# Weights split later and attention steps at new positions, and wide matmuls ahead of narrow ones

## The chip, the cores and the metric

One NeuronCore of a Trainium2 chip runs the whole program in one launch. The metric is the device time of one execution in microseconds; the median of three runs is given, and one execution was profiled.

## The reference

An encoder trunk of two layers on 256 tokens of 1024 channels, in float32. Each layer has a half-step SwiGLU FFN, a token-mixing sub-layer and a second FFN, each between two RMSNorms.

```python
for l in range(DEPTH):                                    # DEPTH = 2
    x = x + 0.5 * rmsnorm(swiglu(rmsnorm(x, g), w_gate, w_up, w_down), g2)   # D_FF = 2816
    x = x + rmsnorm(token_mixing(rmsnorm(x, g), w_in, ..., w_out), g2)
    x = x + 0.5 * rmsnorm(swiglu(rmsnorm(x, g), w_gate, w_up, w_down), g2)

def token_mixing(h, ...):                                 # heads of 64 channels
    qa, ka, va, qb, kb, vb, qc, kc, vc = split(h @ w_in)
    o_a = softmax over a band of chunks + a learned bias  # group A, 6 heads
    o_b = softmax1 - lam * softmax2, then rmsnorm         # group B, 4 heads, lam from 4 small vectors
    o_c = stick-breaking weights                          # group C, 6 heads
    return concat(o_a, o_b, o_c) @ w_out

# stick-breaking: z = q k^T / 8, strictly causal
a = exp(log_sigmoid(z) + reversed_cumsum(log_sigmoid(-z)) - log_sigmoid(-z))
```

## The kernel before

**Precision.** A float32 product is made of three products of float32r halves: every weight chunk is split into `whi` (a cast, on ScalarE, line 139) and `wlo` (raw minus `whi`, on VectorE, line 140), and activations are held as two such halves in `xT`. `mm3` issues high x high, high x low and low x high. In `cols_pair` the two high products are one matmul of 512 columns (`xT` holds both halves side by side, line 405), and the low one is a matmul of 256 columns into the second half of the same PSUM bank (line 407); ScalarE and VectorE then add the halves of the bank.

**The weights' stream.** `Stream` takes the chunks (512 KB as a rule) in the order in which they are used. Four raw buffers are filled by DMAs on SyncE's queue, nine pairs of split buffers hold halves. `stream.ahead(n)` cuts up to `n` half chunks (a cast and a subtraction each), as far as a split buffer is free; when a chunk is cut, its raw buffer is free and the load of the chunk four later is issued. `stream.done()` frees a split pair.

**An FFN.** Two column pairs are done with the tokens on the rows (`gate`, `up`), the nine others with `cols_pair`: gate and up, each with two banks of 8 wide and 8 narrow matmuls. `down` then accumulates 22 chunks into four banks tagged `acc`, three matmuls of 512 columns per product.

**Token mixing.** First the values of the three groups (`values`), then 16 column tiles `pp_0` to `pp_15` of queries and keys (groups B, C, A in turn), each 8 x 3 matmuls of 256 columns, lines 373 to 375. A tile has four quarters of 6 matmuls; quarter q of tile f ends slot 4f + q. After each slot the program issues the steps of the heads that have a position in that slot, and then goes on with the tile. `PLAN` holds these positions, so the order on every engine is written out by this table. The down projection continues the slots from 64 on. The engines run their own instructions strictly in this order and wait for each other by semaphores.

- `qk`: the copy of tile f out of PSUM by ScalarE into `qkT` (`evacuate`, lines 841 and 843).
- `b`: steps of a head of group B: scores `s_b` and softmax for two maps (line 720 on VectorE, 722 on ScalarE), the combination (line 765), transposes `pT_b` on TensorE, their copy `wT_b`, the output `o_b`, its scaling.
- `c`: steps of a pair of heads of group C: scores `s_c` and masked adds (lines 668 and 670) twice, three activations (672 to 674), the combination with the maximum (676) on VectorE, two casts (682, 683) and two differences (684, 685), prefix sums `u_c` on TensorE, two subtractions (697, 698), an exponential (700), the outputs `o_c`, their split `yC`.
- `a`: steps of a pair of heads of group A: scores `s_a`, softmax, scaling, transposes `pT_a`, copies, outputs `o_a`, split.
- `sub`, `turn`, `bias`, `lambda`, `gain`, `table`: the norm of group B's outputs, its transposes, the bias of group A (line 637), lambda (lines 592 to 597), a load and a table of ScalarE.
- `pieces`: entry n is the argument of `stream.ahead` at n + 0.9.
- `acc`: between which positions a PSUM tile of a kind is taken from the `acc` banks (four) and not from the four tagged `rot`, which the column tiles use too.

Of the kernel before, what the change touches and what calls it, by code (L numbers as in the profile page):

```python
# [19 lines left out]
KT = D // P  # L20
# [17 lines left out]

PLAN = {
    "qk": [  # L40
        7.05, 7.1, 14.05, 16.05, 19.05, 23.05, 27.05, 33.05, 35.05, 39.05, 43.05, 47.05, 53.05, 55.05,
        59.05, 63.05
    ],
# [5 lines left out]
    ],  # L49
# [4 lines left out]
    ],  # L54
    "a": [
        [49.1, 49.25, 51.05, 55.05, 57.05, 60.05, 62.05],
        [57.15, 58.35, 59.1, 64.1, 65.05, 68.05, 69.25],
        [65.1, 66.05, 67.05, 72.05, 72.1, 77.05, 78.05],
    ],
    "sub": [  # L60
        55.1, 64.05
    ],
    "turn": [
        [66.15, 66.2],
        [69.2, 69.3],
    ],
    "pieces": [
        1, 0, 0, 1, 2, 0, 3, 0, 0, 2, 1, 0, 2, 0, 0, 4, 0, 0, 0, 4, 0, 0, 2, 2, 2, 1, 0, 2, 4, 3, 1, 1, 1,
        3, 0, 4, 0, 3, 1, 1, 0, 3, 2, 1, 1, 1, 2, 3, 1, 3, 3, 3, 1, 0, 0, 0, 3, 1, 1, 1, 1, 4, 2, 0
    ],  # L70
    "bias": 41.05,
    "lambda": 11.05,
    "gain": 81.1,
    "table": 82.05,
    "tail": 5,
    "acc": {"pT": [14, 26], "oB": [-10, 40], "oC": [-36, -14], "sA": [-140, 58]},
}
NSPLIT = 9

# [82 lines left out]
def trunk_kernel(  # L162
# [55 lines left out]
    stream = Stream(nc, raw_pool, split_pool)  # L218
# [177 lines left out]
    def cols_pair(out, c, nm, between=lambda: None):  # L396

        for j in range(2):  # L400
            cs = slice(j * P, j * P + P)
            ps = psum.tile([P, 2, SEQ], F32, tag="rot", name=f"{nm}_{j}")
            for k in range(KT):
                wh, wl = stream.get(c + k // 4)
                nc.tensor.matmul(ps.rearrange("p a t -> p (a t)"), lhsT=wh[:, k % 4, cs],  # L405
                                 rhs=xT[:, k].rearrange("p a t c -> p (a t c)"), start=k == 0, stop=False)
                nc.tensor.matmul(ps[:, 1, :], lhsT=wl[:, k % 4, cs], rhs=xT[:, k, 0].rearrange("p t c -> p (t c)"),  # L407
                                 start=False, stop=k == KT - 1)
            if j == 0:
                between()  # L410
            side = work.tile([P, 512], F32, tag="tc", bufs=3, name=f"side_{nm}_{j}")[:, :SEQ]
            nc.scalar.copy(side, ps[:, 1, :])  # L412
            nc.vector.tensor_add(out[:, j, :], ps[:, 0, :], side)  # L413
# [54 lines left out]
    def ffn(i, turn1):  # L468
# [74 lines left out]
        for f in range(4, KF, 2):  # L543
            cc = stream.used

            def close():
                while closing:
                    token_close(*closing.pop())

            sg = work.tile([P, 512], F32, tag="ta", bufs=TA, name=f"sg{i}_{f}")  # L550
            cols_pair(sg.rearrange("p (a b) -> p a b", a=2), cc, f"pg{i}_{f}", close)
            nc.scalar.activation(sg, sg, AF.Silu)
            stream.done(2)
            stream.ahead(6)
            h = work.tile([P, 512], F32, tag="tb", bufs=3, name=f"h{i}_{f}")
            hv = h.rearrange("p (a b) -> p a b", a=2)
            cols_pair(hv, cc + 2, f"pu{i}_{f}")
            nc.vector.tensor_mul(h, sg, h)
            split_copy(hT_hi(f, 2), hT_lo(f, 2), hv)
            stream.done(2)  # L560
            stream.ahead(6)
# [13 lines left out]
    def mix(i, l, turn1):  # L575
# [27 lines left out]
        c = stream.used  # L603
# [20 lines left out]
        values(2, 0)  # L624
        values(2, 1)
        stream.done(2)
        stream.ahead(6)
        qkT = act.tile([P, 16, SEQ], F32, tag="bigh1", name=f"qkT{l}")
        yb = act.tile([P, 2816], F32, tag="bigl1", name=f"yb{l}")
        yB = yb[:, :512].rearrange("p (t d) -> p t d", t=2)  # L630
# [298 lines left out]
    for i in range(3 * DEPTH):  # L929
        turn1 = mix(i, i // 3, turn1) if i % 3 == 1 else ffn(i, turn1)  # L930
# [36 lines left out]
```

## Time and profile before

| | |
|---|---|
| median of 3 runs | 1020.4 us (1018.77 to 1021.05) |
| the profiled execution | 1022.65 us |
| its span, first to last instruction | 1020.7 us |
| mean granted clock of TensorE | 0.991 |
| busy: TensorE, VectorE, ScalarE | 996.7, 672.3, 586.4 us |
| loaded | 181.08 MB, 178 GB/s over the span |

Times in rows are microseconds from the span's start. A row of the timeline has start, length, engine, line, operation, tiles, shapes and count, and in brackets how long the engine had been idle and which instruction ended that. "PE" is TensorE's matmuls, "DVE" VectorE, "ACT" ScalarE. A matmul's length includes its drain, so the rows of TensorE overlap, and two starts tell more than one length. The engines' lengths overlap a little, too.

### The profile page before, as it was taken

The numbers are of one execution on the slowest core, as the hardware profiler recorded it, in microseconds if no ns is written. First come the engines' busy times: TensorE is split into PE (matmuls) and PEld (weight loads), VectorE is DVE, ScalarE is ACT, GpSimd is POOL, SyncE is SP. The second block draws the span as 40 slices with busy tenths as digits, with TensorE's granted clock in tenths as the row PEclk, the third lists the DMA queues.
The fourth block names the chain that finished last, engine by engine and source line by source line (L and its number), as shares of the span: only waits on it lengthen the run. The fifth ranks groups of instructions, "written<-read, shape, count | busy, mean of one in ns | idle before, by whom it ended". The sixth has DMA issues, their size and how long they took to land.

```text
span 1020.7 us, 16031 instructions
## 1 busy us (share of the span) xinstructions
PE 996.7 (98%) x5940; PEld 874.6 (86%) x5940; DVE 672.3 (66%) x1345; ACT 586.4 (57%) x1265; POOL 43.2 (4%) x73
## 2 busy tenths in 40 slices
PE   8899999999999999999999999999989999999997
PEld 7788888899887988888899888888978789888886
DVE  4576675577686577765557767646678756866642
ACT  5465564466766566555446756545577655765531
POOL 3100000010000100000020000001000010000000
PEclk8999999999999999999999999999999999999999
DMA  8866656748344477656726865663853525765631
GB/s 265 234 201 181 196 171 228 199 131 235 101 145 124 145 219 217 185 201 210 223 69 206 249 197 173 227 192 118 253 150 105 158 90 175 240 202 189 215 114 41
DMA packets 151005, 183.16 MB, mean 179 GB/s; under 512 B 5744, under 2 KB 134896, under 8 KB 150928
## 3 DMA queue, kind: packets, MB, share of 16 engines
q1 hardware_dynamic: 148448, 174.08, 55.7%
q0 software_dynamic: 2192, 7.54, 2.5%
q8 instruction: 46, 0.75, 0.3%
q10 hardware_dynamic: 288, 0.52, 0.1%
q14 instruction: 31, 0.25, 0.1%
HBM read 181.08 MB, written 1.05 MB: 178 GB/s over the span
## 4 chain that ended last, share of the span: by engine, by line
PE 83%; DVE 5%; DMA 5%; ACT 4%; issue 1%; POOL 0%; SPq 0%; DVEq 0%; POOLq 0%; ACTq 0%
PE pg L405 13%; PE pu L405 13%; PE acc L373 9%; PE acc L375 9%; PE acc L374 9%; PE pg L407 7%; PE pu L407 7%; DVE wlo L140 3%; DMA raw<-in_w_in_dram 2%; PE pp L373 2%; DMA raw<-in_ffn_w_up_dram 2%; PE pp L375 2%; PE pp L374 1%; ACT p_b L722 1%; PE pu L374 1%
## 5 line engine op out<-in xcount | busy, mean ns | idle before, releaser
L140 DVE TENSOR_TENSOR wlo<-raw,whi 128x512 fp32r<-128x512 f32 (+1 forms) x625 | 395.6, 688 | 157.1 <-ACT whi L139 156.8
L139 ACT CAST whi<-raw 128x512 fp32r<-128x512 f32 x630 | 349.8, 617 | 122.0 <-PE acc L375 71.3
L405 PE MATMUL pg<-xT,whi 128*128 128x512 f32 x576 | 207.1, 401 | 0.0
L405 PE MATMUL pu<-xT,whi 128*128 128x512 f32 x576 | 205.2, 399 | 0.0
L407 PE MATMUL pg<-xT,wlo 128*128 128x256 f32 x576 | 162.3, 282 | 0.0
L407 PE MATMUL pu<-xT,wlo 128*128 128x256 f32 x576 | 161.8, 281 | 0.0
L373 PE MATMUL acc<-whi,hh 128*128 128x512 f32 x352 | 137.2, 390 | 0.0
L374 PE MATMUL acc<-wlo,hh 128*128 128x512 f32 x352 | 137.0, 389 | 0.0
L375 PE MATMUL acc<-whi,hl 128*128 128x512 f32 x352 | 137.0, 389 | 0.0
L405 PEld LDWEIGHTS pg<-xT,whi 128*128 128x128 f32 x576 | 108.9, 189 | 26.7
L405 PEld LDWEIGHTS pu<-xT,whi 128*128 128x128 f32 x576 | 108.2, 188 | 27.0
L407 PEld LDWEIGHTS pg<-xT,wlo 128*128 128x128 f32 x576 | 109.5, 190 | 0.0
L407 PEld LDWEIGHTS pu<-xT,wlo 128*128 128x128 f32 x576 | 108.8, 189 | 0.0
L375 PEld LDWEIGHTS acc<-whi,hl 128*128 128x128 f32 x352 | 66.1, 188 | 13.9
L373 PEld LDWEIGHTS acc<-whi,hh 128*128 128x128 f32 x352 | 66.1, 188 | 13.6
L374 PEld LDWEIGHTS acc<-wlo,hh 128*128 128x128 f32 x352 | 66.1, 188 | 13.4
L373 PE MATMUL pp<-xT,whi 128*128 128x256 f32 x256 | 76.4, 298 | 0.0
L374 PE MATMUL pp<-xT,whi 128*128 128x256 f32 x256 | 73.0, 285 | 0.0
L375 PE MATMUL pp<-xT,wlo 128*128 128x256 f32 x256 | 73.0, 285 | 0.0
L412 ACT COPY side_pu<-pu 128x256 f32<-128x256 f32 x72 | 26.1, 368 | 50.3 <-PE pu L407 50.3
L373 PEld LDWEIGHTS pp<-xT,whi 128*128 128x128 f32 x256 | 49.4, 193 | 4.9 <-issue 4.2
L413 DVE TENSOR_TENSOR h<-pu,side_pu 128x256 f32<-128x256 f32 x72 | 29.8, 422 | 30.4 <-ACT side_pu L412 30.2
(247 smaller groups left out, 1455.1 us busy)
## 6 DMA issues: line engine op xcount, KB each, us to landing
raw<-in_ffn_w_gate_dram SPq DMA_DIRECT2D x88, 512.0 KB, 4.8
raw<-in_ffn_w_up_dram SPq DMA_DIRECT2D x88, 512.0 KB, 4.6
raw<-in_ffn_w_down_dram SPq DMA_DIRECT2D x88, 512.0 KB, 4.4
raw<-in_w_in_dram SPq DMA_DIRECT2D x36, 512.0 KB, 5.3
raw<-in_w_out_dram SPq DMA_DIRECT2D x16, 512.0 KB, 3.5
raw<-in_w_in_dram SPq DMA_DIRECT2D x8, 576.0 KB, 4.3
gpost<-in_ffn_post_g_dram POOLq DMA_DIRECT2D x4, 512.0 KB, 4.3
raw<-in_w_in_dram SPq DMA_DIRECT2D x4, 384.0 KB, 3.4
```

Of the source, the lines that this page charges most:

```text
L139: self.nc.scalar.copy(self.hi[:, a:b], raw[:, a:b])
L140: (lo or self.nc.vector).tensor_sub(self.lo[:, a:b], raw[:, a:b], self.hi.bitcast(F32)[:, a:b])
L373: nc.tensor.matmul(ps, lhsT=ah, rhs=bh, start=first, stop=False)
L374: nc.tensor.matmul(ps, lhsT=ah, rhs=bl, start=False, stop=False)
L375: nc.tensor.matmul(ps, lhsT=al, rhs=bh, start=False, stop=last)
L405: nc.tensor.matmul(ps.rearrange("p a t -> p (a t)"), lhsT=wh[:, k % 4, cs], rhs=xT[:, k].rearrange("p a t c -> p (a t c)"), start=k == 0, ...
L407: nc.tensor.matmul(ps[:, 1, :], lhsT=wl[:, k % 4, cs], rhs=xT[:, k, 0].rearrange("p t c -> p (t c)"), start=False, stop=k == KT - 1)
L412: nc.scalar.copy(side, ps[:, 1, :])
L413: nc.vector.tensor_add(out[:, j, :], ps[:, 0, :], side)
L722: nc.scalar.activation(p[:, a:b], p[:, a:b], AF.Exp, bias=st[:, t : t + 1], scale=-1.0, accum_out=st[:, 2 + t : 3 + t])
```

## The change

Three things are changed. In `cols_pair` the 8 wide matmuls of a bank come first and the 8 narrow ones after them. Ahead of the column tiles of token mixing, `stream.ahead(2)` stands for `stream.ahead(6)`. In `PLAN` nearly all positions are new, `pieces` asks for 36 halves where it asked for 88, and the transposes of groups A and B take `rot` banks throughout.

```diff
@@ PLAN
     "qk": [
-        7.05, 7.1, 14.05, 16.05, 19.05, 23.05, 27.05, 33.05, 35.05, 39.05, 43.05, 47.05, 53.05, 55.05,
+        3.05, 7.05, 11.05, 15.05, 19.05, 23.05, 27.05, 31.05, 35.05, 39.05, 43.05, 47.05, 51.05, 55.05,
         59.05, 63.05
     ],
     "b": [
-        [15.02, 15.1, 15.2, 15.3, 15.4, 26.1, 26.25, 30.05, 33.2],
-        [15.05, 15.15, 15.25, 15.35, 15.45, 25.05, 26.05, 33.1, 33.15],
-        [22.05, 22.1, 22.15, 22.2, 22.25, 26.15, 26.2, 30.94, 31.05],
-        [22.07, 22.12, 22.17, 22.22, 22.27, 30.1, 32.05, 44.05, 44.1],
+        [9.1, 9.2, 9.3, 9.4, 9.5, 16.05, 17.05, 20.05, 21.2],
+        [9.12, 9.22, 9.32, 9.42, 9.52, 16.07, 17.07, 20.07, 21.25],
+        [17.1, 17.2, 17.3, 17.4, 17.5, 25.05, 26.05, 29.05, 30.05],
+        [17.12, 17.22, 17.32, 17.42, 17.52, 25.07, 26.07, 29.07, 30.1],
     ],
     "c": [
-        [28.1, 28.15, 28.2, 30.92, 32.1, 39.1, 39.15, 39.2, 42.05, 44.15],
-        [39.25, 39.3, 40.05, 40.1, 44.2, 49.05, 49.15, 49.2, 53.1, 56.05],
-        [43.1, 43.15, 45.05, 45.1, 48.05, 58.05, 58.15, 58.2, 62.15, 62.2],
+        [26.1, 26.15, 26.2, 29.05, 30.15, 34.05, 34.1, 34.15, 38.05, 40.05],
+        [36.1, 36.15, 36.2, 39.15, 40.15, 44.05, 44.1, 44.15, 48.05, 50.05],
+        [45.1, 45.15, 45.2, 48.15, 49.05, 53.05, 53.1, 53.15, 61.05, 62.15],
     ],
     "a": [
-        [49.1, 49.25, 51.05, 55.05, 57.05, 60.05, 62.05],
-        [57.15, 58.35, 59.1, 64.1, 65.05, 68.05, 69.25],
-        [65.1, 66.05, 67.05, 72.05, 72.1, 77.05, 78.05],
+        [50.1, 50.2, 53.2, 56.05, 57.05, 62.05, 63.1],
+        [58.05, 58.2, 60.05, 64.1, 65.05, 68.05, 69.25],
+        [66.05, 66.1, 67.05, 72.05, 72.1, 77.05, 78.05],
     ],
-    "sub": [ 55.1, 64.05 ],
+    "sub": [ 41.1, 46.05 ],
     "pieces": [
...
-    "bias": 41.05,
-    "lambda": 11.05,
+    "bias": 42.05,
+    "lambda": 5.05,
...
-    "acc": {"pT": [14, 26], "oB": [-10, 40], "oC": [-36, -14], "sA": [-140, 58]},
+    "acc": {"pT": [-2, -1], "oB": [-10, 40], "oC": [-36, -14], "sA": [-140, 59]},
@@ cols_pair
             for k in range(KT):
-                wh, wl = stream.get(c + k // 4)
+                wh = stream.get(c + k // 4)[0]
                 nc.tensor.matmul(ps.rearrange("p a t -> p (a t)"), lhsT=wh[:, k % 4, cs],
                                  rhs=xT[:, k].rearrange("p a t c -> p (a t c)"), start=k == 0, stop=False)
+            for k in range(KT):
+                wl = stream.get(c + k // 4)[1]
                 nc.tensor.matmul(ps[:, 1, :], lhsT=wl[:, k % 4, cs], rhs=xT[:, k, 0].rearrange("p t c -> p (t c)"),
                                  start=False, stop=k == KT - 1)
@@ mix
         values(2, 1)
         stream.done(2)
-        stream.ahead(6)
+        stream.ahead(2)
```

The new `pieces` ask for two halves each in the slots 2, 4, 6, 13, 15, 22, 24, 27, 31, 33, 35, 37, 41, 43, 47, 54, 60 and 62, of which the requests of slots 6 and 37 find no free buffer.

On ScalarE, at the start of the column tiles in the first layer, the order before is this (`whi` are casts of weight chunks, `qkT` the copies of column tiles, `lt` the exponential of lambda, `p_b` a softmax of group B):

```order
L139 CAST whi_2361<-raw_2257 128x512 x2
L139 CAST whi_2369<-raw_2291 128x512 x2
L139 CAST whi_2411<-raw_2299 128x512 x2
L841 ACTIVATE qkT_2377<-pp_0_2386 128x256
L843 COPY qkT_2377<-pp_1_2415 128x256
L139 CAST whi_2459<-raw_2307 128x512 x2
L594 ACTIVATE lt_540<-lt_540 128x2
L139 CAST whi_2493<-raw_2367 128x512 x2
L841 ACTIVATE qkT_2377<-pp_2_2446 128x256
L722 ACTIVATE p_b_0_0_2526,st_b_0_0_2527<-p_b_0_0_2526,st_b_0_0_2527 128x128
```

Five chunks and three tiles stood ahead of the first softmax. On the same engine at the same place the order now is this:

```order
L139 CAST whi_2361<-raw_2257 128x512 x2
L139 CAST whi_2397<-raw_2291 128x512 x2
L843 ACTIVATE qkT_2369<-pp_0_2378 128x256
L139 CAST whi_2419<-raw_2299 128x512 x2
L596 ACTIVATE lt_540<-lt_540 128x2
L845 COPY qkT_2369<-pp_1_2412 128x256
L724 ACTIVATE p_b_0_0_2472,st_b_0_0_2473<-p_b_0_0_2472,st_b_0_0_2473 128x128
```

Three chunks, lambda and two tiles stand ahead of it now, and the copy of the second tile stands behind the third chunk and lambda.

On VectorE, from the first to the second pair of group C, the order before is this (`wlo` are low halves of weight chunks, `z_c_0` and `z_c_1` the scores of the first and second pair, `u_c` prefix sums, `s_c` scores in PSUM):

```order
L140 TENSOR_TENSOR wlo_2856<-raw_2611,whi_2855 128x512 x2
L697 TENSOR_TENSOR z_c_0_2756<-z_c_0_2756,u_c_0_2889 128x256
L698 TENSOR_TENSOR z_c_0_2756<-z_c_0_2756,u_c_0_2892 128x512
L668 TENSOR_TENSOR z_c_1_2900<-s_c_1_0_2902,negmask 128x2x128
L670 COPY z_c_1_2900<-s_c_1_0_2902 128x128
L668 TENSOR_TENSOR z_c_1_2900<-s_c_1_1_2907,negmask 128x2x128
L670 COPY z_c_1_2900<-s_c_1_1_2907 128x128
L140 TENSOR_TENSOR wlo_2913<-raw_2695,whi_2912 128x512
L676 SCALAR_TENSOR_TENSOR e_c_1_2901<-z_c_1_2900,e_c_1_2901 128x768
```

The masked adds of the second pair followed the subtractions of the first at once. On the same engine they now stand so:

```order
L140 TENSOR_TENSOR wlo_2820<-raw_2569,whi_2819 128x512 x2
L140 TENSOR_TENSOR wlo_2841<-raw_2696,whi_2840 128x512 x2
L699 TENSOR_TENSOR z_c_0_2744<-z_c_0_2744,u_c_0_2854 128x256
L700 TENSOR_TENSOR z_c_0_2744<-z_c_0_2744,u_c_0_2857 128x512
L140 TENSOR_TENSOR wlo_2873<-raw_2718,whi_2872 128x512 x2
L670 TENSOR_TENSOR z_c_1_2887<-s_c_1_0_2889,negmask 128x2x128
L672 COPY z_c_1_2887<-s_c_1_0_2889 128x128
L670 TENSOR_TENSOR z_c_1_2887<-s_c_1_1_2894,negmask 128x2x128
L672 COPY z_c_1_2887<-s_c_1_1_2894 128x128
L678 SCALAR_TENSOR_TENSOR e_c_1_2888<-z_c_1_2887,e_c_1_2888 128x768
```

Two chunks stand ahead of the subtractions where one stood, and a whole chunk between them and the adds.

More of the change, by code (lines that the diff above doesn't have):

```diff
@@ L44 @@
     "b": [
[4 rows of a table removed]
[4 rows of a table added]
     ],
     "c": [
[3 rows of a table removed]
[3 rows of a table added]
     ],
     "a": [
-        [49.1, 49.25, 51.05, 55.05, 57.05, 60.05, 62.05],
-        [57.15, 58.35, 59.1, 64.1, 65.05, 68.05, 69.25],
-        [65.1, 66.05, 67.05, 72.05, 72.1, 77.05, 78.05],
+        [50.1, 50.2, 53.2, 56.05, 57.05, 62.05, 63.1],
+        [58.05, 58.2, 60.05, 64.1, 65.05, 68.05, 69.25],
+        [66.05, 66.1, 67.05, 72.05, 72.1, 77.05, 78.05],
     ],
     "sub": [
-        55.1, 64.05
+        41.1, 46.05
     ],
@@ L67 @@
     "pieces": [
-        1, 0, 0, 1, 2, 0, 3, 0, 0, 2, 1, 0, 2, 0, 0, 4, 0, 0, 0, 4, 0, 0, 2, 2, 2, 1, 0, 2, 4, 3, 1, 1, 1,
-        3, 0, 4, 0, 3, 1, 1, 0, 3, 2, 1, 1, 1, 2, 3, 1, 3, 3, 3, 1, 0, 0, 0, 3, 1, 1, 1, 1, 4, 2, 0
-    ],
-    "bias": 41.05,
-    "lambda": 11.05,
+        0, 0, 2, 0, 2, 0, 2, 0, 0, 0, 0, 0, 0, 2, 0, 2, 0, 0, 0, 0, 0, 0, 2, 0, 2, 0, 0, 2, 0, 0, 0, 2,
+        0, 2, 0, 2, 0, 2, 0, 0, 0, 2, 0, 2, 0, 0, 0, 2, 0, 0, 0, 0, 0, 0, 2, 0, 0, 0, 0, 0, 2, 0, 2, 0,
+    ],
+    "bias": 42.05,
+    "lambda": 5.05,
     "gain": 81.1,
```

## The prediction

> **What bounds the kernel now.** I read the page's busy times first, then its chain of waits, then the rows of the timeline on the places that the change touches.
>
> ```profile
> PE 996.7 (98%) x5940; PEld 874.6 (86%) x5940; DVE 672.3 (66%) x1345; ACT 586.4 (57%) x1265; POOL 43.2 (4%) x73
> PE 83%; DVE 5%; DMA 5%; ACT 4%; issue 1%; POOL 0%; SPq 0%; DVEq 0%; POOLq 0%; ACTq 0%
> ```
>
> TensorE is the bound (98% busy, 83% of the chain that ended last), so two things count: the spacing of its matmuls, and the places where it waits. Its rows overlap, since each holds its own drain; I therefore read spacing from start to start. These are the first and last rows of a stretch of 12 wide-narrow pairs in the paired columns, of 10 matmuls of 512 columns in the down projection, of 10 of 256 columns in the mixing projection, and the three rows of one prefix sum in which a narrow one, two wide ones and a narrow one follow each other.
>
> ```profile
> 99.73 0.28 PE L407 MATMUL pu<-xT,wlo 128*128 128x256 f32 x1
> 103.97 0.28 PE L407 MATMUL pg<-xT,wlo 128*128 128x256 f32 x1
> ...
> 184.72 0.39 PE L375 MATMUL acc<-whi,hl 128*128 128x512 f32 x1
> 186.98 0.39 PE L373 MATMUL acc<-whi,hh 128*128 128x512 f32 x1
> ...
> 261.76 0.28 PE L374 MATMUL pp<-xT,whi 128*128 128x256 f32 x1
> 262.95 0.28 PE L375 MATMUL pp<-xT,wlo 128*128 128x256 f32 x1
> ...
> 272.07 0.40 PE L691 MATMUL u_c<-h_c,tri 128*128 128x512 f32 x1
> 272.30 0.40 PE L692 MATMUL u_c<-l_c,tri 128*128 128x512 f32 x1
> 272.54 0.39 PE L695 MATMUL u_c<-hl_c,ones_r 128*128 128x256 f32 x2
> ```
>
> A pair in alternation takes (103.97 - 99.73)/12 = 0.353 us. A wide matmul among wide ones takes 2.26/10 = 0.226, a narrow one among narrow ones 1.19/10 = 0.119, together 0.345: alternation costs 0.008 us a pair. At a change of width a wide one takes 0.23 to 0.24, about 0.01 over 0.226.
>
> The other places are the waits of TensorE while the heads run beside the projection, here in the first layer. The first fence has its rows, the second has two windows behind the second wait: stretch, its length, then busy time and instructions of PE, PEld, DVE, ACT and POOL, the granted clock, the DMA share and GB/s.
>
> ```profile
> 249.00 0.28 PE L375 MATMUL pp<-xT,wlo 128*128 128x256 f32 x1
> 250.48 0.53 PE L744 MATMUL s_b<-qkT 32*128 32x128 f32 x8 [1.20 <-ACT qkT L843]
> ...
> 254.78 0.49 PE L729 MATMUL pT_b<-ident,p_b 128*128 128x128 f32 x3
> 257.05 0.74 PE L729 MATMUL pT_b<-ident,p_b 128*128 128x128 f32 x3 [1.78 <-ACT p_b L722]
> ...
> 288.46 0.28 PE L375 MATMUL pp<-xT,wlo 128*128 128x256 f32 x1
> 288.85 0.66 PE L739 MATMUL o_c<-e_c,v 128*64 128x256 f32 x4
> ...
> 291.18 0.49 PE L729 MATMUL pT_a<-ident,p_a 128*128 128x128 f32 x3
> 291.91 0.55 PE L729 MATMUL pT_a<-ident,p_a 128*128 128x128 f32 x3 [0.24 <-ACT qkT L841]
> ```
> ```profile
> 256.00:260.00 4.00, 2.95 (x15) 2.59 (x15) 3.44 (x11) 4.00 (x13) 0.00 (x0) 0.75 0.11 44
> 260.00:264.00 4.00, 4.00 (x30) 3.68 (x30) 2.45 (x6) 1.82 (x4) 0.00 (x0) 0.83 0.62 185
> ```
>
> Start to start less the instruction's own 0.12 (three transposes: 0.33), these waits are 1.36, 1.94, 0.27 and 0.40 us. After the second the clock stood at 0.75 and 0.83 for 4 us each, which is (0.25 + 0.17) x 4 = 1.7 us of work lost. In sum 5.7 us a layer that a better order could give back, and 11.3 over both layers.
>
> **The change part by part.**
>
> *Paired columns.* Per PSUM bank 8 pairs take 8 x 0.353 = 2.83 us. Sorted by width they take 8 x 0.345 = 2.76, and two changes of width add 0.01 each, so 2.78: a gain of 0.046 us. There are 4 FFNs x 9 column pairs x gate and up x 2 = 144 banks: 6.6 us. Its bounds are 0 (if spacing does not depend on the order) and 144 x 0.064 = 9.2 (no price at the changes). I take 6.6, since the prefix sum's rows show that price. The high weight halves are wanted sooner by half a microsecond and the low ones later; no wait stands in any of these rows, and the split runs several chunks ahead, so this costs nothing. If that cover went, the wait would show on the wide matmuls.
>
> In a sentence apart: the Trainium skill, "TensorE: Matmul & The Clock Gate", section "Back-to-back issue gap", gives a gap of N/2.4 + 2.5 ns whatever the neighbour, 216 ns for 512 columns. The trace has 226 and, beside a narrow one, 236 or so, so the rows disagree.
>
> *Splits later.* Counted in the code's tables, 4 halves fewer are cut ahead of the projection, and 36 rather than 88 are asked for during it; the nine buffers grant about as many in both. At the start of a column tile 7 to 9 tiles are still cut ahead, some 20 us of TensorE work (24 matmuls x 0.119 = 2.9 us a tile), so no matmul waits for weights. The loads that each split issues on SP's queue move with it and pass nothing else there. I price this at nothing by itself; what it changes is what stands ahead of the heads' steps on ScalarE and VectorE.
>
> *First heads at slot 9.* A slot is a quarter tile, 6 x 0.119 = 0.72 us. The tiles begin at 231.49, so slot 9 ends at 231.49 + 10 x 0.72 = 238.7. The scores now stand there, and they need the second column tile copied out by ScalarE.
>
> ```profile
> 231.49 0.28 PE L373 MATMUL pp<-xT,whi 128*128 128x256 f32 x1
> ...
> 237.11 1.14 ACT L139 CAST whi<-raw 128x512 fp32r<-128x512 f32 x2 [1.57 <-DMA raw<-in_w_in_dram]
> 238.85 1.14 ACT L139 CAST whi<-raw 128x512 fp32r<-128x512 f32 x2 [0.61 <-DMA raw<-in_w_in_dram]
> 243.22 0.20 ACT L594 ACTIVATE lt<-lt 128x2 f32<-128x2 f32 x1 [1.62 <-DVE lt L593]
> ...
> 242.65 0.29 DVE L592 TENSOR_TENSOR lt<-lt 128x32 f32<-128x32 f32 x2
> 242.97 0.22 DVE L593 TENSOR_REDUCE lt<-lt 128x2 f32<-128x64 f32 x1
> ```
>
> On ScalarE the copy now has the cast of 237.11, the cast of 238.85 and the lambda exponential ahead of it. Both casts wait for a load whose time does not change (the loads ahead of them are issued as before). The second ends at 239.99; VectorE's low half follows to 240.7 (0.60 per half), its two lambda rows take 0.57 up to the exponential as they do at 242.65 to 243.22, so this starts near 241.3 and the copy (0.36) ends at 241.8. TensorE waits 241.8 - 238.7 = 3.1 us. Bounds: 1.2 if the lambda chain were no issue (239.99 - 238.7), 3.5 if loads slip a little. I take 3.1. Such a wait covers most of a clock window; a wait of about 2 us was followed by half clock above, so I add 1.7, together 4.8.
>
> In a sentence apart: the same page, section "Why this matters for your kernels", warns of idle gaps over about 3 us and has the clock fall after one idle window of 3.4 us; the two rows of 0.75 and 0.83 behind a wait of 1.9 us disagree, and by the page the sum below would be up to 3 us smaller.
>
> *The old waits.* From scores at 250.48 to the release of the transposes at 257.05 a softmax took 6.6 us, with four low halves (4 x 0.60) ahead of it on VectorE by the old order. In the new one none stands ahead of the first heads' softmax: 4.2 us for one head and about 1 more for the second, against the score block (0.9) and 7 slots (5.0) up to 16.05. Heads 2 and 3 have one split pair ahead and 8 slots. So the 1.36, 1.94 and their clock loss go; the cover of the first heads is half a microsecond, and would cost what it falls short. The 0.27 and 0.40 are late next again, below.
>
> *The stick-breaking pairs.* Their steps come closer: scores to prefix sum was 10 to 15 slots, now 8, with split pieces between. These rows give the durations (a printed time overlaps the next by some 0.08).
>
> ```profile
> 273.75 0.85 ACT L700 ACTIVATE yb<-z_c 128x768 f32<-128x768 f32 x1 [1.34 <-DVE z_c L698]
> 275.01 0.84 ACT L672 ACTIVATE e_c<-z_c 128x768 f32<-128x768 f32 x1
> 276.75 0.84 ACT L674 ACTIVATE e_c<-e_c 128x768 f32<-128x768 f32 x1
> 279.06 0.41 ACT L682 CAST hl_c<-e_c 128x256 fp32r<-128x256 f32 x1
> 279.37 0.62 ACT L683 CAST h_c<-e_c 128x512 fp32r<-128x512 f32 x1
> ...
> 270.07 1.29 DVE L140 TENSOR_TENSOR wlo<-raw,whi 128x512 fp32r<-128x512 f32 x2 [0.37 <-ACT whi L139]
> 272.96 0.69 DVE L698 TENSOR_TENSOR z_c<-z_c,u_c 128x512 f32<-128x512 f32 x1 [0.27 <-PE u_c L695]
> 273.81 0.42 DVE L668 TENSOR_TENSOR z_c<-s_c,negmask 128x256 f32<-128x256 f32 x1 [0.16 <-PE s_c L665]
> 277.63 0.96 DVE L676 SCALAR_TENSOR_TENSOR e_c<-z_c,e_c 128x768 f32<-128x768 f32 x1 [1.80 <-ACT e_c L674]
> 278.51 0.95 DVE L637 TENSOR_SCALAR yb<-yb 128x1536 f32<-128x1536 f32 x1
> 282.69 0.69 DVE L685 TENSOR_TENSOR l_c<-e_c,h_c 128x512 fp32r<-128x512 f32 x1
> 292.45 0.69 DVE L785 TENSOR_TENSOR sq<-yb 128x512 f32<-128x512 f32 x1
> ```
>
> On TensorE a block of scores, sums or outputs takes 0.9 to 1.0 us, by these rows and the sum that starts at 271.8 and ends with scores at 272.9. Then, instruction by instruction in the new order:
> - First prefix sum (slot 34): from the scores' end 0.9 masked adds, 2.65 three activations, 0.9 copy and first cast, 1.2 low halves, 0.9 the combination, 0.9 two casts, 0.9 two differences with what stands between = 8.35. TensorE has 8 slots, an output block and the first sums: 7.4. Wait 0.95.
> - Second (slot 44): from the last difference of the first, 2.45 two low splits, 0.9 two subtractions, 0.85 exponential, 0.9 copy and cast, 1.2 low split, 1.15 adds, 2.7 activations, 0.9, 0.9 and 0.6 = 12.5. TensorE has 10 slots and three blocks, 10.2. Wait 2.3.
> - Its outputs (slot 48): 1.55 square, sum and scale of the moved norm, 1.2 split, 0.87 the bias, 1.2 split, 0.9 subtractions, 0.85 exponential = 6.55, against 4 slots and 1.6 = 4.45. Wait 2.1.
> - Band scores (slot 50): the third pair's adds and activations end 3.25 after that exponential, against 2.35. Wait 0.9.
> - Third prefix sum (slot 53): 4.25 against 3.5. Wait 0.7. The band transposes (slot 56) inherit about as much, 0.8.
>
> In sum 7.75 us. Bounds from both sides: 0, if what I count as serial is hidden, and 7.75 + 1.7, if the clock falls once more. The adds and casts are in the rows, so I take 7.75. New PSUM banks for the transposes cost nothing: each bank asked for was copied out at least a tile earlier by this walk.
>
> *The sum.* A layer: 4.8 + 7.75 - 5.7 = +6.85, both +13.7; paired columns -6.6; together +7.1 us. The profiled execution took 1022.65 us (span 1020.7, 1.95 around it) and would take 1029.8; it stood 2.25 over the median of 1020.4, so by the median I forecast 1027.5, written 1027.
>
> **The rivals.** A difference of 0.2% (2 us) is about what the measurement can tell.
> - *Only slot 9 waits; faster.* If the pairs' chains hide under TensorE, a layer is 4.8 - 5.7 = -0.9 and the total -1.8 - 6.6 = -8.4: 1012. For it: VectorE is idle a third of the time, and in the old order only 0.27 was lost there. Against it: the chains are serial, and their idle time is between engines. It decides where the waits from slot 34 on sum to less than 4.2 us a layer (4.2 - 0.9 = 3.3, twice is the 6.6 gained). Chance 0.24.
> - *About even.* Half of those waits: -8.4 + 2 x 3.9 = -0.6, 1020. Chance 0.14.
> - *Order of widths does nothing.* The gain of 6.6 falls away: 1034. For it only the skill's gap rule; against it the rows above. Chance 0.08.
> - *The clock.* No fall behind slot 9 (the skill's rule on idle gaps gives this): 3.4 less over both layers, 1024, chance 0.1. One more fall per layer, behind the 2.3 or 2.1 us wait, half of it hidden by the next wait: 1.7 more, 1029, chance 0.1.
>
> **How the numbers follow.** The forecast, all terms about as worked out, has 0.34; with the two clock cases it has 0.54 and a range of its own from 1023 to 1031. Slower by over 0.2% is 0.54 + 0.08 = 0.62, same 0.14, faster 0.24. The range from 1012 to 1034 leaves out a part of the faster case (waits under 3 us from slot 34 on, or a gain nearer 9) and the upper half of the widths' case, together under 0.2.
>
> **What the new profile would show.** Wide starts 0.226 apart in the paired columns and 16 matmuls in 2.78 us. TensorE waiting at the first scores for ScalarE's copy near slot 9, about 3 us, and a window of half clock behind it in each layer; no wait at the second heads' scores. Then waits on u_c and o_c of the second pair, of about 2 us each. I am wrong if the wait at slot 9 is under 1.5 us, or the u_c and o_c waits of a layer together under 2.

## The result: slower, 1032.0 us after 1020.7

Over four runs each the medians are 1032.04 us for the changed kernel (1031.1 to 1032.32) and 1020.72 for the one before (1020.4 was the median of the three runs that the forecast started from). The ratio is 1.0115, with a 95% interval from 1.0096 to 1.0133. The profiled executions differ by 9.5 us (spans of 1030.2 and 1020.7): the one of before stood above its median, the one of the changed kernel stands on it.

The page's busy line of the changed kernel says little: TensorE is the bound as before, at 97%.

```profile
PE 1000.5 (97%) x5940; PEld 881.0 (86%) x5940; DVE 672.7 (65%) x1345; ACT 586.7 (57%) x1265; POOL 43.7 (4%) x73
```

What tells is the starts on TensorE. These rows of the timelines are the first matmul of the column tiles and the first of the down projection behind them: before, then after, the first layer and then the second in each.

```profile
231.49 0.28 PE L373 MATMUL pp<-xT,whi 128*128 128x256 f32 x1
...
301.99 0.39 PE L373 MATMUL acc<-whi,yC 128*128 128x512 f32 x1
...
728.90 0.28 PE L373 MATMUL pp<-xT,whi 128*128 128x256 f32 x1
...
799.56 0.39 PE L373 MATMUL acc<-whi,yC 128*128 128x512 f32 x1
```
```profile
230.56 0.28 PE L373 MATMUL pp<-xT,whi 128*128 128x256 f32 x1
...
308.90 0.39 PE L373 MATMUL acc<-whi,yC 128*128 128x512 f32 x1
...
733.23 0.28 PE L373 MATMUL pp<-xT,whi 128*128 128x256 f32 x1
...
810.37 0.39 PE L373 MATMUL acc<-whi,yC 128*128 128x512 f32 x1
```

The column tiles with the heads took 70.50 and 70.66 us and now take 78.34 and 77.14: 14.3 us more. All else went from 1020.7 - 141.2 = 879.5 to 1030.2 - 155.5 = 874.7: 4.8 us less.

The waits of TensorE in the changed kernel come next: line, what was waited for, total, number, longest.

```profile
PE s_b L746 <- ACT qkT L845: 6.7, 2, 3.9
PE u_c L690 <- ACT hl_c L684: 3.4, 2, 1.7
...
PE o_c L741 <- ACT e_c L702: 2.6, 2, 2.1
```

The old waits of `pT_b` for the softmax are gone. The scores of the first heads wait for ScalarE's copy, the second pair's prefix sum for its casts, its outputs for the exponential. The rows below come from the timeline of the first layer: the first scores; the first matmul of the prefix sum, and the column tile's matmul that follows the whole sum; the outputs. The last two rows are the outputs and the first scores in the second layer.

```profile
237.65 0.28 PE L375 MATMUL pp<-xT,wlo 128*128 128x256 f32 x1
241.87 0.53 PE L746 MATMUL s_b<-qkT 32*128 32x128 f32 x8 [3.94 <-ACT qkT L845]
...
279.50 0.28 PE L375 MATMUL pp<-xT,wlo 128*128 128x256 f32 x1
281.50 0.38 PE L690 MATMUL u_c<-hl_c,tri 128*128 128x256 f32 x1 [1.71 <-ACT hl_c L684]
...
283.32 0.28 PE L373 MATMUL pp<-xT,whi 128*128 128x256 f32 x1
...
288.62 0.28 PE L375 MATMUL pp<-xT,wlo 128*128 128x256 f32 x1
289.45 0.66 PE L741 MATMUL o_c<-e_c,v 128*64 128x256 f32 x4 [0.55 <-ACT e_c L702]
...
790.93 0.66 PE L741 MATMUL o_c<-e_c,v 128*64 128x256 f32 x4 [2.06 <-ACT e_c L702]
...
743.33 0.53 PE L746 MATMUL s_b<-qkT 32*128 32x128 f32 x8 [2.74 <-ACT qkT L845]
```

Start to start less the row's own 0.12, in the first layer the first scores waited 4.1 us, the prefix sum 1.9 ahead of it and 0.8 inside it (1.82 against 1.03 for the undisturbed one before), the outputs 0.7.

The granted clock stands in the windows, behind the counts of five engines; the fourth and fifth rows are from the second layer:

```profile
240.00:244.00 4.00, 2.13 (x21) 1.76 (x22) 2.76 (x15) 1.19 (x5) 0.00 (x0) 0.83 0.82 226
244.00:248.00 4.00, 4.00 (x28) 4.00 (x27) 3.14 (x20) 4.00 (x17) 0.00 (x0) 0.74 0.22 62
284.00:288.00 4.00, 4.00 (x23) 3.39 (x23) 3.96 (x9) 0.31 (x1) 2.43 (x2) 0.62 0.35 96
...
744.00:748.00 4.00, 4.00 (x27) 3.78 (x20) 2.82 (x20) 3.27 (x15) 0.00 (x0) 0.57 0.57 157
792.00:796.00 4.00, 4.00 (x22) 3.19 (x22) 2.12 (x5) 2.89 (x5) 0.00 (x0) 0.57 0.37 142
```

Behind the first scores (0.17 + 0.26) x 4 = 1.7 us of work are lost in the first layer, and 0.43 x 4 = 1.7 in the second. In this execution the clock fell a second time in each layer: behind the prefix sum (0.38 x 4 = 1.5 in the window shown) in the first and behind the outputs (0.43 x 4 = 1.7) in the second. The execution of before has one fall a layer; this is its second:

```profile
756.00:760.00 4.00, 4.00 (x22) 3.39 (x21) 3.50 (x9) 2.24 (x6) 0.00 (x0) 0.57 0.43 113
```

Two falls more, at 1.7 us each, are thus 3.4 of the 14.3 us.

In the paired columns the runs of one width now stand merged; these rows are one bank's wide run and narrow run, and the start of the next bank.

```profile
101.22 2.00 PE L405 MATMUL pg<-xT,whi 128*128 128x512 f32 x8
103.06 1.11 PE L409 MATMUL pg<-xT,wlo 128*128 128x256 f32 x8
104.01 2.00 PE L405 MATMUL pg<-xT,whi 128*128 128x512 f32 x8
```

A bank takes 2.79 us. The narrow run's 0.95 is 8 x 0.119; the wide run's 1.84 is 0.03 over 8 x 0.226.

### The profile page after: what moved, and what is told of

Its sections match the earlier page's. It is cut to its first block, busy times and chain, and to the rows that moved or that the text cites. A ratio compares the mean times of both kernels' runs of the same rounds, so it can differ in the third digit from the quotient of the medians.

```text
span 1030.2 us, 16032 instructions
## 1 busy us (share of the span) xinstructions
PE 1000.5 (97%) x5940; PEld 881.0 (86%) x5940; DVE 672.7 (65%) x1345; ACT 586.7 (57%) x1265; POOL 43.7 (4%) x73
## 4 chain that ended last, share of the span: by engine, by line
PE 84%; DVE 6%; ACT 5%; DMA 3%; issue 1%; POOL 0%; SPq 0%; DVEq 0%; POOLq 0%; ACTq 0%
PE pg L405 13%; PE pu L405 13%; PE acc L373 9%; PE acc L375 9%; PE acc L374 9%; PE pg L409 7%; PE pu L409 7%; DVE wlo L140 3%; DMA raw<-in_ffn_w_gate_dram 2%; PE pp L373 2%; PE pp L374 2%; PE pp L375 2%; PE pg L373 1%; PE pg L375 1%; PE pg L374 1%; PE pu L373 1%
## 5 line engine op out<-in xcount | busy, mean ns | idle before, releaser
L405 PE MATMUL pg<-xT,whi 128*128 128x512 f32 x576 | 146.5, 397 | 0.0
L405 PE MATMUL pu<-xT,whi 128*128 128x512 f32 x576 | 144.2, 392 | 0.0
L405 PEld LDWEIGHTS pg<-xT,whi 128*128 128x128 f32 x576 | 104.7, 191 | 18.8
L405 PEld LDWEIGHTS pu<-xT,whi 128*128 128x128 f32 x576 | 103.6, 189 | 18.5
L409 PEld LDWEIGHTS pg<-xT,wlo 128*128 128x128 f32 x576 | 79.4, 192 | 5.7
L409 PEld LDWEIGHTS pu<-xT,wlo 128*128 128x128 f32 x576 | 78.6, 190 | 5.6
L409 PE MATMUL pg<-xT,wlo 128*128 128x256 f32 x576 | 81.1, 284 | 0.0
L409 PE MATMUL pu<-xT,wlo 128*128 128x256 f32 x576 | 80.3, 282 | 0.0
L373 PE MATMUL pp<-xT,whi 128*128 128x256 f32 x256 | 77.7, 303 | 0.0
L374 PE MATMUL pp<-xT,whi 128*128 128x256 f32 x256 | 74.5, 291 | 0.0
L373 PEld LDWEIGHTS pp<-xT,whi 128*128 128x128 f32 x256 | 50.8, 199 | 5.1 <-issue 4.5
L374 PEld LDWEIGHTS pp<-xT,whi 128*128 128x128 f32 x256 | 51.1, 200 | 0.0
```

The source lines that it names most:

```text
L373: nc.tensor.matmul(ps, lhsT=ah, rhs=bh, start=first, stop=False)
L374: nc.tensor.matmul(ps, lhsT=ah, rhs=bl, start=False, stop=False)
```

## The experiments

The times of before beside them are medians of 1020.1 (first four) and 1020.3 us (last four). One thing has to be kept apart in every comparison: how often the clock fell in the column tiles with the heads, at 1.7 us a time. In the profiled executions that is twice in the kernel before, four times in the changed kernel, and 0, 3, 1, 3, 0, 3, 3 and 2 times in e1 to e8.

**e1: the order of widths alone.** The kernel before with the new `cols_pair`.

```diff
             for k in range(KT):
-                wh, wl = stream.get(c + k // 4)
+                wh = stream.get(c + k // 4)[0]
                 nc.tensor.matmul(... wide ...)
+            for k in range(KT):
+                wl = stream.get(c + k // 4)[1]
                 nc.tensor.matmul(... narrow ...)
```

> The old token mixing with the new order in the paired columns alone. Theory (the changed kernel's trace has 2.797 us a bank against 2.830): 144 x 0.033 = 4.8 us less than before, 1014.5 to 1017.5 us. Rival (the order of widths does nothing by itself, the shorter banks come from the changed mixing): as before, 1019 to 1022 us.

Measured: 1015.17 us, ratio 0.9952 (0.9933 to 0.9971), 5 us less than before. This part is a gain by itself, of the size that the banks show. In the profiles, all that lies outside the column tiles with the heads went from 879.5 to 874.8 us; the tiles themselves went from 141.2 to 137.5, nearly all of it the two falls of the clock that this execution does not have.

**e2: the positions and the later splits alone.** The changed kernel with the old `cols_pair`.

> The new positions and the later splits alone, with wide and narrow matmuls alternating as before. Theory (each wait comes from the queue right ahead of it in token mixing and has nothing to do with the paired columns): the changed kernel plus 4.8, 1035 to 1039 us, waits as in the changed kernel. Rival (the faster columns bring TensorE too early to the mixing and make part of the waits): 1030 to 1033 us.

Measured: 1037.41 us, ratio 1.0167 (1.0139 to 1.0195). That is 17 us over before and 5 over the changed kernel, so the two parts add up. Its waits are close to those of the changed kernel: 5.9 us in total of the scores for `qkT` (6.7 there), 3.4 of the prefix sum for `hl_c` and 2.6 of the outputs for `e_c` (the same). The 0.8 us do not speak for the rival: e4, e6 and e7 below have the new `cols_pair` and the same work at slot 9, and their scores waited 6.3, 5.6 and 5.8.

**e3: lambda out of the way, and a split that was meant to be.**

```diff
-    "lambda": 5.05,
+    "lambda": 7.1,
     "pieces": slot 4: 2 -> 0, slot 10: 0 -> 2
```

> The changed kernel with lambda at 7.1 and one chunk's split moved from slot 4 to slot 10, so that one cast less and not lambda's exponential stand ahead of the second tile's copy. Theory (ScalarE's queue ahead of that copy makes the wait at slot 9): the wait falls from 4.0 and 2.8 us to under 0.8, no half clock behind it, 1021 to 1026 us. Rival (the loads set it, whatever stands in the queue): the wait stays over 2.3 us, 1029 to 1032. Second rival (the split only moves the wait): no wait at the first scores, but as much at the next transposes or scores, 1029 to 1032.

Measured: 1024.94 us, ratio 1.005 (1.0033 to 1.0068). The time came out in the range of the theory, the wait did not: the scores still waited 1.84 us in the first layer, with a fall of the clock behind it. The request of slot 6, which finds no buffer in the changed kernel, now found one and cut the chunk there. ScalarE's timeline shows its cast still ahead of the second copy, and lambda's exponential behind it:

```profile
235.82 1.14 ACT L138 CAST whi<-raw 128x512 fp32r<-128x512 f32 x2 [0.35 <-DMA raw<-in_w_in_dram]
236.87 0.36 ACT L844 COPY qkT<-pp 128x256 f32<-128x256 f32 x1
238.26 0.20 ACT L595 ACTIVATE lt<-lt 128x2 f32<-128x2 f32 x1 [1.03 <-DVE lt L594]
```
```profile
237.29 0.53 PE L745 MATMUL s_b<-qkT 32*128 32x128 f32 x8 [1.84 <-ACT qkT L844]
```

So e3 tells apart only lambda: without it the wait was 1.4 to 2.1 us shorter. The 7 us cannot be put down to that. The mixing held one fall of the clock where the changed kernel had four, which is 5.1 of the 6.1 us by which it is shorter in the profiles (155.5 to 149.4). The second pair's prefix sum waited 1.2 us less a layer, since one chunk and not two stood ahead of the first pair's subtractions on VectorE. The outputs behind it waited longer, 4.1 us in total against 2.6:

```profile
PE o_c L740 <- ACT e_c L701: 4.1, 2, 2.1
```

e5 moves the split as it was meant.

**e4: the old positions of the pairs.** The changed kernel with `c`, `a`, `sub` and `bias` of the kernel before.

> The changed kernel with the old positions of the stick-breaking pairs, the band pairs, the norm of group B and the bias; the new positions of tiles, group B, lambda and splits stay. Theory (the close positions of the pairs make the waits from slot 34 on, 7 to 8 us a layer with the clock): 1016 to 1022 us, the wait at slot 9 as before it. Rival (ScalarE and VectorE have too much to do by then in sum, since splits come later, and the waits move with the positions): 1026 to 1032 us.

Measured: 1020.22 us, 12 less than the changed kernel, of which one fall of the clock less is 1.7 in the profiles. That is 5.9 a layer, less than the 7 to 8 expected. Against before the ratio is 1.0005 (0.9992 to 1.0018). The waits of `u_c` on ScalarE are gone, that of `o_c` is small, and the first scores wait as long as ever:

```profile
PE s_b L746 <- ACT qkT L845: 6.3, 2, 3.4
...
PE o_c L741 <- ACT e_c L702: 0.9, 2, 0.5
```

ScalarE and VectorE do as much with the late splits in this run (586.6 and 672.2 us busy; 586.7 and 672.7 in the changed kernel), so it is the four entries put back, not the sum of the work, that made the waits from slot 34 on.

**e5: both mended.** e4 with lambda at 7.1, one split at slot 10, and nothing at slots 4 and 6.

```diff
-    "lambda": 5.05,
+    "lambda": 7.1,
     "pieces": slots 4 and 6: 2 -> 0, slot 10: 0 -> 2
```

> Old positions of the pairs (as in e4), lambda at 7.1, and the split of slot 4 at slot 10 with the request of slot 6 taken out (in e3 that request took the chunk up instead, so the cast still stood ahead of the copy). Theory (ScalarE's queue makes the wait at slot 9): 3.5 us of wait a layer in e4 fall under 0.8 and the half clock behind them goes: 1020.2 less 8 to 10, 1010 to 1013 us, below both kernels and below e1's 1015.2. Rival (what is moved comes back as a wait of the first transposes at slot 16): 1015 to 1019 us.

Measured: 1013.37 us (1010.73 to 1015.58), ratio 0.9935 (0.9915 to 0.9955). This is just over the 1010 to 1013 of the theory, and beats both kernels, by 7 and 19 us; e1, at 1015.17, is too near to be told from it. The copy now follows the one before it on ScalarE at once, the scores start 0.2 us late, and there was no fall of the clock in the mixing (two in the kernel before, four in the changed one):

```profile
238.38 0.38 ACT L842 ACTIVATE qkT<-pp 128x256 f32<-128x256 f32 x1
238.66 0.36 ACT L844 COPY qkT<-pp 128x256 f32<-128x256 f32 x1
240.30 0.20 ACT L595 ACTIVATE lt<-lt 128x2 f32<-128x2 f32 x1 [1.28 <-DVE lt L594]
```
```profile
238.74 0.28 PE L374 MATMUL pp<-xT,wlo 128*128 128x256 f32 x1
239.07 0.53 PE L745 MATMUL s_b<-qkT 32*128 32x128 f32 x8
```

What the rival said came true in a small part: of the wait, 0.5 us a layer came back at the transposes of the first heads.

```profile
PE pT_b L730 <- ACT qkT L842: 1.0, 2, 0.5
```

**e6: the norm of group B back.** The changed kernel with `"sub": [55.1, 64.05]`.

> The changed kernel with the norm of group B's outputs back at 55.1 and 64.05. Theory (the norm's 1.55 us on VectorE stand ahead of the second pair's subtractions, so the wait for its outputs at slot 48 holds them): that wait falls by about 1.5 us from 1.1 to 2.2 a layer, and 1027 to 1030 us in all. Rival (VectorE has slack there and the wait is set by the splits and the bias alone): no change, 1031 to 1033 us.

Measured: 1029.66 us, ratio 1.0087 (1.0065 to 1.011), 2.4 less than the changed kernel. This time alone would prove little, since in the profiles one fall of the clock less is 1.7 us. The wait does: that of the outputs fell from 2.6 to 1.0 us in total:

```profile
PE o_c L741 <- ACT e_c L702: 1.0, 2, 0.5
```

The norm stood ahead of the subtractions; it was one of the four things there, with two splits and the bias.

**e7: one split from slot 35 to slot 40** (and the request of slot 37 out).

> The changed kernel with one chunk's split moved from slot 35 to slot 40, behind the second pair's casts (the request of slot 37, which would take it up, is taken out). Theory (this split stands ahead of the second pair's masked adds, so it is 1.85 us of the 2.7 us that the second prefix sum waits): that wait falls to about 0.9, but the split then stands ahead of the norm and the outputs' wait at slot 48 grows by about 1.2, so 0 to 3 us less in all, 1029 to 1032 us. Rival (the wait comes from the activations' length, not the split): the wait stays at 2.4 us or more.

Measured: 1026.29 us, ratio 1.0057 (1.0038 to 1.0076). The wait of the prefix sum went altogether, and the outputs' wait rose to 3 us in each layer, so the split moved from one wait to the next. These are the last part of the sum and the outputs on TensorE, and then what stands on VectorE between them:

```profile
279.61 0.39 PE L696 MATMUL u_c<-hl_c,ones_r 128*128 128x256 f32 x2
...
286.91 1.11 PE L740 MATMUL o_c<-e_c,v 128*64 128x256 f32 x4 [2.98 <-ACT e_c L701]
```
```profile
278.86 1.29 DVE L139 TENSOR_TENSOR wlo<-raw,whi 128x512 fp32r<-128x512 f32 x2
280.07 0.68 DVE L786 TENSOR_TENSOR sq<-yb 128x512 f32<-128x512 f32 x1
...
281.61 1.30 DVE L139 TENSOR_TENSOR wlo<-raw,whi 128x512 fp32r<-128x512 f32 x2
282.84 0.95 DVE L638 TENSOR_SCALAR yb<-yb 128x1536 f32<-128x1536 f32 x1
283.71 1.28 DVE L139 TENSOR_TENSOR wlo<-raw,whi 128x512 fp32r<-128x512 f32 x2
284.91 0.41 DVE L698 TENSOR_TENSOR z_c<-z_c,u_c 128x256 f32<-128x256 f32 x1
```

The sum's last part ends by 279.61 + 0.39 = 280.0, and the subtraction that needs it starts at 284.9: three splits, the norm (its first row is shown) and the bias, 6 us without a gap, stand ahead of it. The gain of 5.7 us is more than the 0 to 3 that I expected of the move. In the profiles the mixing is 4.6 us shorter (155.5 to 150.9): 1.7 is one fall of the clock less, in the second layer, 0.9 a shorter wait of the first scores, which the move does not touch, and only the 2 us that are left are the exchange of the one wait for the other.

**e8: blocks of four.** The kernel before with four wide, four narrow, four wide and four narrow matmuls a bank.

> The old token mixing with blocks of four wide and four narrow matmuls, twice a bank, in place of eight and eight (e1). First theory (the extra time over 2.776 us a bank, which the changed kernel's trace shows on the second to fifth wide matmul, belongs to the bank's start, when ScalarE and VectorE read the bank before): as e1, 2.79 to 2.80 us a bank and 1014 to 1017 us. Second (it belongs to the matmuls behind a change of width): 2.81 to 2.82 us a bank, 1017 to 1019 us.

Measured: 1017.59 us, ratio 0.9971 (0.9958 to 0.9984). A bank, from its first wide run to the next bank's, takes 103.94 - 101.14 = 2.80 us in these rows:

```profile
101.14 1.09 PE L406 MATMUL pg<-xT,whi 128*128 128x512 f32 x4
102.07 0.63 PE L410 MATMUL pg<-xT,wlo 128*128 128x256 f32 x4
102.54 1.09 PE L406 MATMUL pg<-xT,whi 128*128 128x512 f32 x4
103.47 0.64 PE L410 MATMUL pg<-xT,wlo 128*128 128x256 f32 x4
103.94 1.09 PE L406 MATMUL pg<-xT,whi 128*128 128x512 f32 x4
```

Both wide runs of four take 0.93 us, 0.23 a matmul, so the extra time is not at the bank's start alone. Over the whole trace a bank takes 2.807 us on average (2.795 in e1), so bank and time fit the second theory better than the first. But a second change of width in a bank added only about 0.01 us, where the first costs 0.03; why the wide matmuls behind narrow ones are slower is left open.

## Why the prediction was right, and where its terms were off

I forecast 1027 us, slower, with a range of 1012 to 1034; 1032.0 was measured. The way and the two places of the loss came out as worked out; the narrower range of 1023 to 1031, of the forecast and its clock cases, just missed.

- *First heads at slot 9.* I gave 3.1 us of wait and 1.7 of clock; measured 4.1 and 2.9 (the second layer's scores start at 743.33, the matmul ahead of them at 740.31), and 1.7 in each layer. The 4.1 is the longest of its kind: in e2, e4, e6 and e7, with the same work at slot 9, this wait was 2.7 to 3.5. e3 and e5 show the cause that was named: ScalarE's queue ahead of the copy, a cast and lambda each holding a part. The lower bound of 1.2 without lambda left out the copy itself; e3 has 2.0 and 1.4.
- *The old waits go.* They did: no wait of `pT_b` for the softmax is left.
- *The pairs.* The second prefix sum was to wait 2.3 us and waited 1.9 + 0.8 = 2.7; its outputs 2.1, measured 0.7 in the first layer, where the half clock ahead of them took up 1.5, and 2.2 in the second. e6 and e7 show that the norm and a split stand in these waits, and e4 that the waits on ScalarE's casts go with the old positions.
- *The sum of the mixing.* 13.7 forecast, 14.3 measured. That this is so near is partly luck. It holds a second fall of the clock in each layer, 3.4 us in all, to which I gave a chance of 0.1; against that, the waits from slot 34 on come to some 6.5 us a layer, start to start, where 7.75 were forecast.
- *Paired columns.* This term was mis-sized: 6.6 forecast, 4.8 measured (144 x 0.033; e1 and e2 give 5 in the times). The 4.8 outside the mixing in the two profiles is no second proof: there the changed kernel's execution lost 8.0 us to the clock against 5.9, and its listed waits are 8.8 us against 11.0, and the two differences happen to cancel. The step was "two changes of width add 0.01 each": the prefix sum's rows show what one wide matmul costs beside a narrow one, but behind the change several run at about 0.23 (1.84 us for eight, and 0.93 for four in e8).
- *From profile to median.* I took the changed kernel's profiled execution to stand 2.25 over its median, as the one of before did. Nothing spoke for that, and it stands on it: this is half of the 4.5 us that the forecast was low by. e1 shows what can make such a difference: its profiled execution has the old wait of the transposes, with the clock at 1.00 behind it, where before had 0.75 and 0.83.

```profile
255.04 0.74 PE L731 MATMUL pT_b<-ident,p_b 128*128 128x128 f32 x3 [1.77 <-ACT p_b L724]
```
```profile
256.00:260.00 4.00, 4.00 (x36) 3.72 (x35) 3.51 (x9) 2.65 (x7) 0.00 (x0) 1.00 0.34 66
```

The record has the mean granted clock of every execution, and it goes with the time: of the 38 executions of the kernel before in the experiments, the three at 0.989 took 1022.3 to 1023.4 us, the four at 0.994 took 1016.5 to 1021.0, and 0.001 of the span is 1.0 us. So one and the same kernel loses more to the clock in some executions than in others.

Of the rivals, "only slot 9 waits" and "about even" fell: the waits from slot 34 on summed to over 4.2 us a layer. Of the clock's two, the one with a second fall in each layer is what happened in the profiled execution. "The order of widths does nothing" fell with e1. The Trainium skill gives the gap of an isolated matmul by its number of columns alone ("TensorE: Matmul & The Clock Gate", section "Back-to-back issue gap"), which would make both orders equal; banks of 2.83 us before and 2.79 in e1 disagree. The Trainium skill's warning of gaps over 3 us (same page, section "Why this matters for your kernels") is no bound here: the clock fell behind waits of 1.9 and 2.2 us.

## What to carry to other kernels

With engines that run in order, a wait is worked out from the queue ahead of the instruction that is waited for: add up what stands there, from the order and the durations of the trace, and compare with the work of the bound engine between the two points. Splits and casts that are free by their total are not free at a given place; put them behind the short chains, and look where each lands when a request finds no buffer. A change that moves many things may hold a gain and a loss: take it apart before it is dropped, since here one half alone (e1), and the changed kernel with the pairs put back and lambda and one split moved (e5), beat both kernels. And count the falls of the clock before a difference is put down to a wait: in e3 they were most of it.

## What the runs showed of the hardware

A wait of TensorE of 1.8 to 2 us was followed by half clock in the kernel before (0.75 and 0.83 in two windows of 4 us) and by none in e1 (1.00). The first scores waited 2.7 to 4.1 us ten times in five profiles (the changed kernel, e2, e4, e6, e7), and the clock fell each time, during the wait or right behind it; the outputs' waits of 3.0 us in e7 were followed by a fall in the first layer and by none in the second. In windows of half a microsecond a fall shows as a clock of 0.50 for about 3.4 us, so it costs about 1.7 us of work. Matmuls of 512 columns run every 0.226 us among their like, about 0.234 when each stands between narrow ones (0.353 less 0.119), and about 0.23 in runs of four and eight behind narrow ones.
